# Down products of two FFN blocks in one PSUM group: one read-out for two blocks, two sets of operands

## The chip, the cores and the metric

The kernel runs on one core of one Trainium2 chip. The metric is the device time of one execution in microseconds (us); the median of several runs is quoted. The core's engines are TensorE (PE in the profile, with its weight loads shown apart as PEld), VectorE (DVE), ScalarE (ACT), GpSimd (POOL) and SyncE (SP, which here only issues DMAs). Each engine works through its own queue in order, and waits in it for semaphores of the others.

## The reference, cut to what matters

A trunk of two layers over 1024 positions and 1024 channels. Each layer first mixes tokens (Fourier groups, a linear recurrence and neighbourhood attention, not touched here) and then runs a SwiGLU feed-forward network (FFN) whose gated result is added to x:

```
h = modulate(rms_norm(x, g_ffn[l]), sh2, sc2)
f = (silu(h @ w_ffn_gate[l]) * (h @ w_ffn_up[l])) @ w_ffn_down[l]
x = x + gt2 * f
```

The inner width is 2816, that is 22 blocks of 128. Block number f contributes the product of a 128-column slice of silu(gate) * up, called A below, with 128 rows of `w_ffn_down`.

## The kernel before, in words

x stands transposed in SBUF as 8 tiles of 128 channels by 1024 positions. Every fp32 matmul is made of three matmuls on operands that were split into a rounded high part (hi) and a remainder (lo): hi by hi, hi by lo, lo by hi (`mm3`). A split costs one ACT copy (hi) and one subtraction on DVE, or for some weights on POOL (lo).

**FFN, blocks 0 and 1** are computed plainly by 16 jobs (`e_job`) of 12 matmuls each; the last four of them call `e_hook` after every sixth matmul, eight times in all. Meanwhile DVE and ACT prepare combinations of the normalised input (`prep`), with temporaries in the tile FA2 of the pool "prep".

**FFN, blocks 2 to 21** get gate and up from seven products in place of eight (`p_job`, in the order p = 1, 5, 6, 2, 7, 3, 4): 7 jobs of 12 matmuls, 84 in a block. The weights of p = 5, 6, 7 and 3 are combinations that POOL makes of the raw gate weights (wg) and up weights (wu). A job's weights are combined and split three jobs ahead, into a ring of four slots. The raw weights of the next block are loaded by two DMAs of 512 KB, issued with the preparation of p = 4. After each job `after` adds the product's bank into temporaries on DVE; after p = 3 and p = 4 the two halves (512 positions each) of A are complete, and `a_split` splits them.

**The down products.** `hook` is called after every sixth matmul, 14 times in a block. At eight of these hooks it calls `down_pair(l, f, m)` for one of the eight 128-channel tiles m of x: six matmuls for the block before, three into each of two PSUM banks (one for each half of the positions), and then one `scalar_tensor_tensor` (L204) of 128 by 1024 on DVE that multiplies both banks by the gate gt2 and adds them to x. The bank pairs 0-1 and 2-3 take turns; banks 4 to 7 belong to the seven products. The pairs of block f - 1 run at hooks 2 to 6 and 8 to 10 of block f, so that gate matmuls and down matmuls alternate by sixes. A block thus has 84 + 48 = 132 matmuls. There is one set of operands, A and its counterpart DW (the split rows of `w_ffn_down`), in the pool "ffa"; A of block f is written over that of block f - 1 once the latter's pairs are through. The rows of `w_ffn_down` come in two DMAs of 256 KB a block (`dw_load`) through one raw buffer, and `dw_split` splits each. The pairs of block 0 run in `e_hook` and the first hooks of block 2, those of block 1 behind them. Blocks 20 and 21 have their down products after the loop (`down_tail`), which adds both blocks up in PSUM already; block 21 keeps its operands in HX.

**Beside it, in layer 0,** blocks 3 to 16 compute layer 1's modulation vectors in the background: at each hook `bg(1)` advances `half_steps` by one step, and two steps are one DMA of 256 KB of `w_ada` into a single buffer (L1479) and one multiply-and-reduce over it on DVE (L1481, called the reduce below). Seven such pairs fall in a block.

Only PE's order is that of the code. The queues of the other engines are put in order when the program is built, by priority and by when operands are expected.

## Time and profile before

| | |
|---|---|
| time, median of 3 runs | 2391.38 us (2387.48 to 2394.67) |
| the profiled execution's own time | 2383.19 us |
| its span | 2381.3 us |
| mean granted TensorE clock | 0.974 |
| PE, PEld busy | 2236.1 us (94%), 1792.0 us (75%) |
| DVE, ACT, POOL busy | 1861.6 us (78%), 972.5 us (41%), 779.2 us (33%) |

The span runs from the first to the last instruction of the profiled execution; its own time is 1.9 us longer. Shares are of the span. The FFN of layer 0 with its down products lies at about 550 to 1208 us of the span, that of layer 1 at about 1715 to 2359 us.

### The profile page before, as it was taken

How to read it: one execution, taken by the hardware profiler on the slowest of the kernel's cores; microseconds unless marked ns; L12 is line 12 of the kernel's file. 1: busy time of each engine (PE TensorE's matmuls, PEld its weight loads, DVE VectorE, ACT ScalarE, POOL GpSimd, SP SyncE). 2: the span in 40 equal slices, each digit the busy share in tenths (PEclk: the TensorE clock that was granted, in tenths of full speed). 3: DMA queues.
4: the chain of work that ended last, by engine and by line, in shares of the span. 5: the costliest groups of instructions: out<-in, count | busy, mean ns of one | idle time of the engine just before them, and what ended most of it. 6: DMA issues, size and time to landing. Idle time of an engine off the chain costs nothing.

```text
span 2381.3 us, 27260 instructions
## 1 busy us (share of the span) xinstructions
PE 2236.1 (94%) x9802; PEld 1792.0 (75%) x9802; DVE 1861.6 (78%) x2698; ACT 972.5 (41%) x1606; POOL 779.2 (33%) x570
## 2 busy tenths in 40 slices
PE   6887998999999999999989989899999999999996
PEld 4665876777777778788867777677778888888885
DVE  8888788788788888887765676987877777777775
ACT  5375475543222222222353746745422222222234
POOL 4224375202233333333230325740123233333333
PEclk9998999999999999999989999999999999999998
DMA  8323423321333333321221132323011111111112
GB/s 294 101 72 107 137 74 123 116 99 45 98 107 110 112 113 102 113 74 53 80 97 58 40 107 69 110 73 118 27 58 54 54 52 51 49 50 53 53 49 71
DMA packets 77423, 203.81 MB, mean 86 GB/s; under 512 B 8932, under 2 KB 13028, under 8 KB 77287
## 3 DMA queue, kind: packets, MB, share of 16 engines
q1 hardware_dynamic: 73540, 183.41, 23.8%
q10 hardware_dynamic: 3746, 18.66, 2.3%
q8 instruction: 77, 1.26, 0.2%
q14 instruction: 60, 0.48, 0.1%
HBM read 193.64 MB, written 8.39 MB: 85 GB/s over the span
## 4 chain that ended last, share of the span: by engine, by line
PE 71%; DVE 17%; issue 4%; ACT 3%; POOL 2%; DMA 2%; SPq 0%; POOLq 0%; ACTq 0%; DVEq 0%
PE psum L190 71%; DVE rounded L201 3%; DVE plain L201 2%; DVE plain L204 1%; DVE ffa_A L201 1%; DVE psum L885 1%; DVE plain L312 1%; DMA plain<-in_ada 1%; ACT plain L198 1%; DVE psum L201 1%; ACT rounded L198 1%; ACT ffa_A L198 1%; ACT lru_LF L198 1%; POOL plain L1576 1%; DVE lru_LF L693 1%
## 5 line engine op out<-in xcount | busy, mean ns | idle before, releaser
L190 PE MATMUL psum<-rounded 128*128 128x512 f32 (+2 forms) x4332 | 1061.2, 394 | 34.2 <-DVE rounded L201 9.7
L190 PEld LDWEIGHTS psum<-rounded 128*128 128x128 f32 (+1 forms) x4332 | 817.2, 191 | 212.9 <-DVE rounded L201 12.6
L204 DVE SCALAR_TENSOR_TENSOR plain<-psum,plain 128x1024 f32<-128x1024 f32 (+2 forms) x416 | 474.7, 1148 | 202.2 <-PE psum L190 199.9
L198 ACT ACTIVATE rounded<-plain 128x512 fp32r<-128x512 f32 (+3 forms) x428 | 283.6, 668 | 743.9 <-PE psum L190 643.5
L190 PE MATMUL psum<-ffa_A,ffa_DW 128*128 128x512 f32 (+1 forms) x2040 | 526.7, 392 | 15.7 <-DVE ffa_A L201 6.7
L1323 POOL TENSOR_TENSOR plain<-plain 128x512 f32<-128x512 f32 x160 | 224.4, 1403 | 735.9 <-DMA plain<-in_wu 384.7
L190 PEld LDWEIGHTS psum<-ffa_A,ffa_DW 128*128 128x128 f32 x2040 | 378.8, 189 | 112.7 <-DVE ffa_A L201 16.3
L190 PE MATMUL psum<-hx_HX,rounded 128*128 128x512 f32 x1488 | 382.9, 394 | 0.0
L190 PEld LDWEIGHTS psum<-hx_HX,rounded 128*128 128x128 f32 x1488 | 280.4, 188 | 62.1
L1339 POOL TENSOR_TENSOR rounded<-plain,rounded 128x512 fp32r<-128x512 f32 x120 | 172.2, 1435 | 289.3 <-ACT rounded L198 289.1
L201 DVE TENSOR_TENSOR plain<-psum,plain 128x512 f32<-128x512 f32 (+1 forms) x288 | 193.9, 686 | 23.7 <-PE psum L190 16.4
L201 DVE TENSOR_TENSOR rounded<-plain,rounded 128x512 fp32r<-128x512 f32 (+4 forms) x147 | 154.5, 1065 | 50.1 <-ACT rounded L198 47.4
L922 POOL TENSOR_TENSOR rounded<-qk_PE,rounded 128x512 fp32r<-128x512 f32 (+3 forms) x132 | 140.8, 1074 | 127.7 <-ACT rounded L198 92.2
L198 ACT ACTIVATE plain<-plain 128x512 f32<-128x512 f32 (+5 forms) x181 | 113.3, 634 | 90.5 <-DVE plain L201 52.9
L190 PE MATMUL psum<-rounded,v_V 128*65 128x512 f32 (+4 forms) x528 | 130.1, 361 | 13.5 <-ACT rounded L198 3.6
L201 DVE TENSOR_TENSOR plain<-plain 128x512 f32<-128x512 f32 (+5 forms) x156 | 134.3, 863 | 6.9 <-ACT plain L198 1.9
L190 PE MATMUL psum<-qk_QT 128*128 128x512 f32 (+8 forms) x432 | 109.6, 354 | 22.1 <-DVE plain L885 16.4
L1339 DVE TENSOR_TENSOR rounded<-plain,rounded 128x512 fp32r<-128x512 f32 x160 | 115.5, 722 | 5.4 <-ACT rounded L198 5.3
L190 PEld LDWEIGHTS psum<-rounded,v_V 128*65 128x65 f32 (+1 forms) x528 | 75.4, 152 | 52.0 <-POOL rounded L922 6.3
L201 DVE TENSOR_TENSOR psum<-psum,plain 128x256 f32<-128x256 f32 x240 | 97.7, 410 | 21.1 <-PE psum L190 14.3
L198 ACT ACTIVATE ffa_DW<-plain 128x512 fp32r<-128x512 f32 x84 | 53.0, 631 | 139.2 <-PE psum L190 137.4
L190 PEld LDWEIGHTS psum<-qk_QT 128*128 128x128 f32 (+1 forms) x432 | 75.4, 194 | 41.4 <-DVE plain L885 20.4
(128 smaller groups left out, 2046.0 us busy)
## 6 DMA issues: line engine op xcount, KB each, us to landing
plain<-in_ada SPq DMA_DIRECT2D x96, 256.0 KB, 2.7
plain<-in_wd SPq DMA_DIRECT2D x88, 256.0 KB, 2.5
plain<-in_wg SPq DMA_DIRECT2D x40, 512.0 KB, 3.5
plain<-in_wu SPq DMA_DIRECT2D x40, 512.0 KB, 3.7
plain<-in_ada SPq DMA_DIRECT2D x30, 512.0 KB, 3.5
start_AT<-in_ada SPq DMA_DIRECT2D x18, 512.0 KB, 5.7
plain<-in_bias_t ACTq DMA_DIRECT2D x12, 768.0 KB, 5.8
plain<-in_bias_s ACTq DMA_DIRECT2D x12, 736.0 KB, 4.2
```

Source lines behind the costliest of these rows:

```text
L190: self.nc.tensor.matmul(out=out, lhsT=lhsT, rhs=rhs, start=start, stop=stop)
L198: self.nc.scalar.activation(out=out, in_=in_, func=func, **kw)
L201: self.nc.vector.tensor_tensor(out=out, in0=a, in1=b, op=op)
L204: self.nc.vector.scalar_tensor_tensor(out=out, in0=a, scalar=s, in1=b, op0=op0, op1=op1)
L312: self.nc.vector.tensor_tensor_reduce(out=raw, in0=raw, in1=self.f(self.M0, U), op0=ALU.mult, op1=ALU.add, scale=1.0, scalar=0.0, accum_ou ...
L693: nc.vector.tensor_tensor_scan(out=t, data0=a, data1=i, initial=0.0, op0=ALU.mult, op1=ALU.add)
L885: self.nc.vector.tensor_tensor_reduce(out=s, in0=s, in1=self.f(bo, a * w).rearrange("p (a b) -> p a b", a=a), op0=ALU.add, op1=ALU.max, sc ...
L922: (self.nc.vector if PLAN[self.l]["lo"][self.step] else self.nc.gpsimd).tensor_tensor(out=pl, in0=p, in1=ph.bitcast(F32), op=ALU.subtract)
L1323: comb = lambda out, a, b, op=ALU.subtract: nc.gpsimd.tensor_tensor(out=out, in0=a, in1=b, op=op)
L1339: (nc.gpsimd if LO_ENG[p] else nc.vector).tensor_tensor(out=lo, in0=src, in1=hi.bitcast(F32), op=ALU.subtract)
L1576: self.nc.gpsimd.tensor_tensor(out=x, in0=x, in1=accs[0], op=ALU.mult)
```

## The change

The down products of two neighbouring blocks, an even one and the odd one behind it, now go into one accumulation group: `down_pair(l, f, m)` issues twelve matmuls (for each half of the positions three of block f and three of block f + 1 into the same bank) and one `scalar_tensor_tensor` for both blocks. All of a pair's work stands in the next even block, at its hooks 3 to 10 (4 to 11 in block 2); odd blocks have none. An even block then has 84 + 96 = 180 matmuls and an odd one 84. There are two sets of operands: A0 and DW0 for even blocks, A1 and DW1 for odd ones. A1 and DW1 take the place of FA2, which is now put at the other end of SBUF and given up at the first hook of block 2. The loads and splits of the `w_ffn_down` rows keep their number but move: an even block splits the first half of its own rows, and an odd block the first half of its own, the second half of the even block's and the second half of its own. Blocks 0 and 1 no longer have down products in `e_hook`.

```diff
-PAIRS = {2: 0, 3: 1, 4: 2, 5: 3, 6: 4, 8: 5, 9: 6, 10: 7}
+PAIRS = {i + 3: i for i in range(8)}, {i + 4: i for i in range(8)}
...
-        self.pp = self.open(f"prep{l}", FA2=(4 * U, F32))
+        self.pp = self.open(f"prep{l}", "right", FA2=(4 * U, F32))
...
-            self.ap = self.open(f"ffa{l}", A=(2 * U, F32R), DW=(2 * U, F32R))
+            self.ap = self.open(f"ffa{l}", A0=(2 * U, F32R), DW0=(2 * U, F32R))
...
-        if i >= 4:
-            self.down_pair(l, 0, i - 4)
-        if i == 4:
+        elif i == 4:
             self.dw_split(0, 1)
             self.dw_load(l, 1, 0)
-        elif i == 7:
-            self.dw_split(1, 0)
-            self.dw_load(l, 1, 1)
...
     def ad(self, f):
-        return (self.HX[:, :2 * U], self.HX[:, 2 * U:4 * U]) if f == NRUN - 1 else (self.A[:, :], self.DW[:, :])
+        if f == NRUN - 1:
+            return self.HX[:, :2 * U], self.HX[:, 2 * U:4 * U]
+        return (self.A1, self.DW1) if f % 2 else (self.A0, self.DW0)
...
     def down_pair(self, l, f, m):
         d = self.fd()
         for j, n in enumerate(NS):
-            self.down(f, m, n, self.bank(d + j), True, True)
+            for i in range(2):
+                self.down(f + i, m, n, self.bank(d + j), not i, i == 1)
...
         if f == FIRST:
-            if i < 4:
-                self.down_pair(l, 0, 4 + i)
-            if i == 3:
-                self.dw_split(1, 1)
+            if i == 0:
+                self.shut(self.pp)
+                self.pp = self.open(f"ffb{l}", "right", A1=(2 * U, F32R), DW1=(2 * U, F32R))
+                self.dw_split(1, 0)
+                self.dw_load(l, 1, 1)
+            elif i == 1:
                 for half in range(2):
                     self.e_split(1, half)
                 self.free.append(self.ea[1, 0])
+            elif i == 2:
+                self.dw_split(1, 1)
                 self.dw_load(l, f, 0)
-            m = i - 4
-            prev = 1
-        else:
-            m = PAIRS.get(i, -1)
-            prev = f - 1
+        elif f % 2 == 0:
             if i == 0:
                 self.dw_load(l, f, 0)
...
+        m = -1 if f % 2 else PAIRS[f == FIRST].get(i, -1)
+        if m >= 0:
+            self.down_pair(l, f - 2, m)
             if m == 3:
                 self.dw_split(f, 0)
-                self.dw_load(l, f, 1)
-            if m == 7:
-                self.dw_split(f, 1)
-        if self.late and i >= LATE:
+                self.dw_load(l, f + 1 if f + 1 < NRUN - 1 else f, f + 1 == NRUN - 1)
+        if f % 2 and f < NRUN - 1:
+            if i in (1, 5, 9):
+                self.dw_split(f - (i == 5), i > 1)
+                if i < 9:
+                    self.dw_load(l, f - (i == 1), 1)
```

## Rows read from the trace of the kernel before

**Rows 1.** The page: busy time, share of the span, instructions of two engines
```profile
PE 2236.1 (94%) x9802; PEld 1792.0 (75%) x9802; DVE 1861.6 (78%) x2698; ACT 972.5 (41%) x1606; POOL 779.2 (33%) x570
```

**Rows 2.** Windows: eleven blocks of layer 0, eleven of layer 1, block 21 of layer 0
```profile
core 0: us, PE busy (x) PEld busy (x) DVE busy (x) ACT busy (x) POOL busy (x), PEclk, DMA share, GB/s
671.15:1015.65 344.50, 338.97 (x1452) 271.96 (x1453) 297.31 (x442) 93.66 (x155) 112.51 (x77) 1.00 0.35 110
1829.90:2162.60 332.70, 332.70 (x1453) 271.84 (x1452) 248.88 (x276) 94.59 (x155) 105.63 (x77) 1.00 0.17 53
1163.55:1182.81 19.26, 19.26 (x86) 15.78 (x84) 12.36 (x17) 9.41 (x14) 3.36 (x3) 1.00 0.40 123
```

**Rows 3.** Waits of PE, 671.15 to 1015.65, then 1710 to 2320 (total us, times, longest)
```profile
PE psum L190 <- ACT ffa_A L198: 3.0, 11, 0.5
PE psum L190 <- DVE ffa_A L201: 2.5, 11, 0.3
...
PE psum L190 <- DVE ffa_A L201: 1.9, 2, 1.2
PE psum L190 <- DVE plain L204: 1.7, 1, 1.7
```

**Rows 4.** Timeline of PE: first down matmuls of blocks 4 and 7, layer 0
```profile
638.29 0.50 PE L190 MATMUL psum<-ffa_A,ffa_DW 128*128 128x512 f32 x1 [1.67 <-ACT ffa_A L198]
639.02 1.61 PE L190 MATMUL psum<-ffa_A,ffa_DW 128*128 128x512 f32 x5 [0.22 <-DVE ffa_A L201]
640.43 2.76 PE L190 MATMUL psum<-hx_HX,rounded 128*128 128x512 f32 x6
642.99 1.79 PE L190 MATMUL psum<-ffa_A,ffa_DW 128*128 128x512 f32 x6
...
733.75 0.50 PE L190 MATMUL psum<-ffa_A,ffa_DW 128*128 128x512 f32 x1 [0.24 <-ACT ffa_A L198]
734.47 1.42 PE L190 MATMUL psum<-ffa_A,ffa_DW 128*128 128x512 f32 x5 [0.22 <-DVE ffa_A L201]
```

**Rows 5.** Timeline of DVE at the end of one block, layer 0
```profile
761.10 0.68 DVE L201 TENSOR_TENSOR plain<-psum,plain 128x512 f32<-128x512 f32 x1
761.88 1.00 DVE L201 TENSOR_TENSOR ffa_A<-plain,ffa_A 128x512 fp32r<-128x512 f32 x1
762.80 1.77 DVE L201 TENSOR_TENSOR plain<-plain 128x512 f32<-128x512 f32 x1
764.50 0.68 DVE L1481 CUSTOM_DVE_ANT_0 plain<-plain 128x512 f32<-128x512 f32 x1
...
765.27 0.69 DVE L201 TENSOR_TENSOR ffa_A<-plain,ffa_A 128x512 fp32r<-128x512 f32 x1
```

**Rows 6.** Groups of DVE, 671.15 to 1015.65 (count | busy us, mean ns | idle before)
```profile
L204 DVE SCALAR_TENSOR_TENSOR plain<-psum,plain 128x1024 f32<-128x1024 f32 x88 | 112.1, 1280 | 17.2 <-PE psum L190 17.0
L1481 DVE CUSTOM_DVE_ANT_0 plain<-plain 128x512 f32<-128x512 f32 x77 | 58.3, 758 | 21.4 <-DMA plain<-in_ada 20.8
```

**Rows 7.** Two reduces in a row on DVE; landing times of the DMAs before them
```profile
737.18 0.69 DVE L1481 CUSTOM_DVE_ANT_0 plain<-plain 128x512 f32<-128x512 f32 x1 [1.76 <-DMA plain<-in_ada]
...
740.45 0.69 DVE L1481 CUSTOM_DVE_ANT_0 plain<-plain 128x512 f32<-128x512 f32 x1 [0.18 <-DMA plain<-in_ada]
...
DMA to landing us min/median/max: 2.4/2.7/3.5
```

**Rows 8.** Timeline of PE, then DVE, while blocks 0 and 1 end, layer 0
```profile
553.18 1.44 PE L190 MATMUL psum<-ffa_A,ffa_DW 128*128 128x512 f32 x5 [0.65 <-DVE ffa_A L201]
...
565.91 1.63 PE L190 MATMUL psum<-ffa_A,ffa_DW 128*128 128x512 f32 x6 [1.66 <-DVE plain L204]
...
579.57 0.72 PE L190 MATMUL psum<-ffa_A,ffa_DW 128*128 128x512 f32 x2 [1.22 <-DVE ffa_A L201]
...
566.29 1.39 DVE L201 TENSOR_TENSOR rounded<-prep_FA,rounded 128x512 fp32r<-128x512 f32 x1
```

**Rows 9.** Timelines of ACT, SP and POOL: raw up weights on their way, layer 0
```profile
742.66 0.64 ACT L198 ACTIVATE rounded<-plain 128x512 fp32r<-128x512 f32 x1 [4.89 <-PE psum L190]
...
748.17 0.33 SPq L1258 DMA_DIRECT2D plain<-in_wu  x1
...
752.45 3.13 POOL L1323 TENSOR_TENSOR plain<-plain 128x512 f32<-128x512 f32 x2 [13.31 <-DMA plain<-in_wu]
755.54 1.29 POOL L1339 TENSOR_TENSOR rounded<-plain,rounded 128x512 fp32r<-128x512 f32 x1
```

More of the change, by code (lines that the diff above doesn't have):

```diff
@@ L152, in __init__, with open @@
         self.queue, self.look, self.sq = deque(), 1, {}
-    def open(self, name, **tiles):
-        cm = self.tc.tile_pool(name=name, bufs=1)
+    def open(self, name, side="left", **tiles):
+        cm = self.tc.tile_pool(name=name, bufs=1, side=side)
         pool = cm.__enter__()
```

18 lines of the change are left out of this document (9 added, 9 removed).

## Prediction

> **What bounds the kernel now.** I read the page's engine shares first. PE is busy 94% of the span and DVE 78% [rows 1]: PE is the bound, and DVE work costs time only where PE waits for it. The change takes no matmul away, so anything it brings must come out of PE's waits. So the next view was PE's waits, one FFN at a time.
>
> The windows say where they are. Eleven whole blocks of layer 1 take 332.70 us with PE busy in all of it, that is 30.25 us a block. Eleven of layer 0 take 344.50 us, 31.32 us a block, with the same number of matmuls and the full granted clock [rows 2]. Layer 0 loses 1.07 us a block. The waits name the place: eleven times PE waits for ACT's and eleven times for DVE's half of the split of A [rows 3], at the first down pair of a block. The timeline shows one such place: 0.24 and 0.22 us idle, and the matmuls behind them start late as well [rows 4]. DVE's timeline shows why A is late: add the last product (761.10), split the other half, a multiplication that takes 1.77 us, then a background reduce at 764.50, and the last subtraction ends at 765.96 [rows 5]. Layer 1 has no reduces and no such wait.
>
> So the places where the change can pay are the entries of layer 0's blocks 4 to 16, thirteen of them, and the start of each FFN, where PE idles 0.65, 1.66 and 1.22 us in layer 0 [rows 8] and 3.6 us in layer 1 [rows 3].
>
> **What is removed.** Eight pairs for two blocks instead of sixteen: 80 fewer evacuations a layer, 160 in all, at 1.280 us [rows 6], 205 us of DVE. In layer 1 this hides entirely behind PE, which never waited in its steady blocks: worth 0 there.
>
> **What moves: the entries of blocks.** A of an even block f is now needed two blocks later, so the six entries of odd blocks (5 to 15) lose their wait. At an even block's entry A of the odd block before is still needed, but later: at hook 3 instead of 2 (6 matmuls), and behind 3 matmuls of the even block's half, 9 matmuls at 0.229 us (332.70 us over 1453, [rows 2]) or 2.06 us. The present loss is 1.07 us, so 1.0 us is to spare.
>
> What the 13 entries cost now: twelve at 1.07 are 12.8 us. The first (block 4) is dearer: 1.67 us idle; then 2.14 us from 638.29 to 640.43, and 2.56 from there to 642.99, for six matmuls each that take 1.37 elsewhere [rows 4]: 1.67 + 0.77 + 1.19 = 3.6. Together 16.4 us.
>
> **What is added: odd blocks without cover.** An odd block has only its 84 matmuls. Block 21 of layer 0 is such a block in the present trace: 19.26 us, PE busy throughout [rows 2], but without reduces and without a next block's weights. That is 0.229 us a matmul, so alternating with down matmuls costs nothing that its end would give back. DVE's work in an odd block of layer 0 is 297.31 / 11 = 27.0 us less eight evacuations (10.2), plus a third `w_ffn_down` split (0.7, like the subtraction at 765.27, [rows 5]): 17.5 us of 19.26. To that come waits for the w_ada DMAs, 20.8 / 11 = 1.9 us a block now [rows 6]: 19.4 us, just full.
>
> These waits can grow. The reduces come every second hook, 12 matmuls or 2.75 us in an odd block; two in a row can't start closer than about 3.27 us (737.18 to 740.45, where the second waited for its DMA, which needs 2.4 us at the least, [rows 7]). Seven need 22.9 us, 3.6 more than the block has. How much of this delays A depends on whether DVE stands waiting in its queue or has other work first. Bounds for the added wait at each of the seven even entries (4, 6, ... 16): below, all absorbed, 0; above, all 3.6 us less the 1.0 to spare, 2.6 us, 18.2 in all. With the waits of today A would be 0.1 us late, inside the slack; with twice the waits, 21.3 us, 2.0 us late, 1.0 beyond it. I take the middle, 0.5 us, 3.5 in all: reduces now mostly run behind other work, as the one at 764.50 did. Layer 0's entries then give 16.4 - 3.5 = 12.9 us (bounds 16.4 and -1.8).
>
> **The multiplication** of 1.77 us [rows 5] reads two SBUF operands while the add of the same size from PSUM takes 0.68. The Trainium skill's page "SBUF — State Buffer", section "Who interferes with whom", says that a DVE instruction with two SBUF inputs contends with a GpSimd instruction that reads SBUF, and one with a single SBUF input does not; the trace agrees with 1.77 against 0.68. By that rule the evacuations never disturbed POOL, so removing them frees nothing there, while the same POOL work in a shorter odd block meets DVE's two-input work more often: another multiplication drawn out by 1.1 us each time would be 7.7 us over seven blocks, within the bounds above.
>
> **Start of each FFN.** The down pairs of block 0 leave the stretch at 552 us, so the three waits (0.65, 1.66, 1.22 us) lose their place: block 0's A has five more hooks, the 1.66 us for a late evacuation [rows 8] has no evacuation left to wait for, and A1 isn't written over A0, which put the 1.22 us there. Late next is A1 and DW1 themselves: they lie where FA2 was, and the preparation reads FA2 until 567.7 (566.29 plus 1.39, [rows 8]). Without the three evacuations in that stretch of DVE it would end at 567.7 - 3 x 1.28 = 563.9. From 552.2, the hook of the first pair now, to the new first pair at hook 4 of block 2 lie eight groups of six gate matmuls, 1.37 us each: 563.1, and 563.8 behind the three matmuls of A0. A split of DW1 and one of A1 follow the release: 2 x 0.69 on DVE behind 0.64 on ACT, 565.9 at the latest. Wait 0 to 2.1 us, taken as 1.0. Each layer saves 3.5 to 3.6 less 1.0: 2.5, two layers 5.0 us (bounds 2.9 and 7.1).
>
> **At nothing:** the loads keep their number and size (256 KB each for `w_ffn_down`) and their raw buffer has 12 or more matmuls between uses, 2.75 us against the 2.4 to 2.7 us that DMAs of this size take [rows 7]; uncovered, each would cost ACT 1 to 2 us in its queue, ahead of weight splits that are made three jobs (8.2 us) early. A bank pair is used again two hooks later, 5.5 us with gate work, against 1.28 us for the evacuation. The tail is unchanged.
>
> **Sum.** 12.9 + 5.0 = 17.9 us. From the profiled execution's own 2383.2 us this makes 2365.3. That execution was 8.2 us quicker than the median of the runs, 2391.4; on that scale the forecast is 2373.5 us, 0.75% less.
>
> **Rivals.**
> 1. *All absorbed.* DVE keeps up in odd blocks, and A1 is in time: 16.4 + 7.1 = 23.5 us, 2368. For it: evacuations are 10.2 of DVE's 27.0 us a block. Against it: 17.5 of 19.26 us are still booked, with waits to come.
> 2. *The reduces take the place of the evacuations.* All 2.6 us at the seven entries: layer 0 gives -1.8, the starts 5.0; 3.2 us gained, 2388: no change. For it: 1.76 us of such waiting stands in the trace with two evacuations ready behind it or nearly so [rows 7]. Close to it is the case that nothing at all is gained, 2391: PE is busy 94%, and work is taken from an engine that isn't the bound. The Trainium skill's page "Perfetto Trace Analysis", section "Identifying the Most-Contended Engine", says to find the engine with the highest occupancy and to optimise that one first; by that rule a cut in DVE's work gives 0. The trace disagrees in part: PE waits for DVE at the places counted above.
> 3. *The weights become late in odd blocks: slower.* The raw up weights of the next block can be asked for only when p = 4 of this one is split. Now that split begins at 742.66 on ACT, the DMA is issued at 748.17, 5.5 us later, and POOL has combined and split the first product from them by 756.83, 8.7 us after that [rows 9]. In an odd block the split can begin after three jobs, 8.2 us in; 8.2 + 5.5 + 8.7 = 22.4 us, and PE wants it at 19.26 + 2.75 = 22.0. It decides as soon as the DMA goes out later than 13.3 us into an odd block. If the 3.6 us by which the reduces lag come on top, PE waits 4.0 us in each of seven blocks: 28.0 us lost, against 17.9: 10.1 us slower, 2401.5. Against it: the 5.5 us hold evacuations that are gone from odd blocks; each is 1.28.
>
> **How the numbers follow.** Forecast 0.50, rival 1 0.18, rival 2 with its neighbour 0.21, rival 3 0.11. About 0.3% (7.2 us) is what a measurement of this kernel can tell from no change; the three runs of before lie as far apart. Faster 0.68, same 0.21, slower 0.11. The likeliest case's own range is 2368 to 2382 (the wait at even entries between 0 and 1.4 us, A1's between 0 and 2.1). The range of 2365 to 2393 reaches over rivals 1 and 2 and leaves out rival 3 and the edges.
>
> **What would show it.** Right: 160 fewer evacuations; no wait for A at odd entries of layer 0; even entries with under 1 us; PE's start waits below 1.1 us a layer; pairs of blocks in layer 0 at 60.5 to 62 us, in layer 1 unchanged at 60.5. Wrong: PE waiting for weight splits (`rounded`) of the first products of even blocks would be rival 3; waits for A of 2 us and more at even entries, with DVE idle for w_ada before them, rival 2. A new order of the queues that holds up something I didn't look at would make it wrong in either direction.

## The result, and the profile after

The changed kernel takes 2402.73 us, median of 7 runs (2396.42 to 2405.36), against 2388.54 us (2384.50 to 2394.67, 7 runs) of the kernel before: ratio 1.0058, 95% interval 1.0046 to 1.0070. It is slower by 14 us; a gain of 0.75% was forecast.

The profiled execution has an own time of 2400.51 us, 17.3 above that of before. Matched matmul by matmul, 5.6 us of this lie ahead of 550 us, where both kernels issue the same matmuls: from 510.8 us TensorE's granted clock stands at 1.2 GHz for 13.7 us, in the execution of before for 3.4 us. Both lengths turn up in executions of either layout, so this part is not the change's. The start of layer 0's FFN wins 0.5 us, 11.8 are lost in layer 0's blocks 3 to 16, and all that follows comes to 0.4.

The page's engine line, to be held against [rows 1]:
```profile
PE 2247.8 (94%) x9802; PEld 1805.0 (75%) x9802; DVE 1689.2 (70%) x2538; ACT 965.0 (40%) x1606; POOL 780.0 (33%) x570
```
DVE has 160 instructions and 172 us less; PE as many matmuls as before. The windows of ten blocks of layer 0 (from the entry of block 6, its first down matmul, to that of block 16) and ten of layer 1, against [rows 2]:
```profile
core 0: us, PE busy (x) PEld busy (x) DVE busy (x) ACT busy (x) POOL busy (x), PEclk, DMA share, GB/s
698.05:1019.30 321.25, 310.77 (x1321) 252.00 (x1320) 236.39 (x370) 84.55 (x141) 103.43 (x71) 0.98 0.36 110
1867.59:2170.46 302.87, 302.81 (x1322) 247.78 (x1320) 178.75 (x211) 83.70 (x142) 95.79 (x70) 1.00 0.17 53
```
Layer 1 takes 60.57 us for two blocks, as before (60.5). Layer 0 takes 64.25, where before had 62.64: each even entry now costs 3.68 us, against 2.14 for two entries before. Of the 18.38 us that layer 0 takes more than layer 1 here, 10.48 are idle PE; 7.9 are not idle, and the clock column shows 0.98.

PE's waits in 580 to 1060 us, then in layer 1, against [rows 3]:
```profile
PE psum L190 <- ACT ffb_A L198: 14.5, 7, 3.3
PE psum L190 <- DVE ffb_A L201: 1.8, 6, 0.7
...
PE psum L190 <- ACT ffb_A L198: 1.6, 1, 1.6
PE psum L190 <- DVE ffb_A L201: 1.2, 1, 1.2
```
Odd blocks have no wait left, as forecast. The seven even ones wait 16.3 us, all for `ffb_A`, the A1 of the odd block before. Layer 1 waits only at its start, 2.8 us where it was 3.6. PE's timeline at the entry of block 12 (some expectations below call it block 10's), against [rows 4], and the windows of the same place:
```profile
889.53 0.86 PE L190 MATMUL psum<-ffa_A,ffa_DW 128*128 128x512 f32 x3
893.04 1.95 PE L190 MATMUL psum<-ffb_A,ffb_DW 128*128 128x512 f32 x3 [2.64 <-ACT ffb_A L198]
894.78 1.49 PE L190 MATMUL psum<-ffa_A,ffa_DW 128*128 128x512 f32 x3
...
890.00:893.00 3.00, 0.39 (x2) 0.00 (x0) 2.93 (x7) 0.65 (x2) 0.37 (x1) 1.00 0.74 191
893.00:896.50 3.50, 3.46 (x8) 2.43 (x9) 1.81 (x3) 1.51 (x3) 1.27 (x1) 0.52 0.39 136
896.50:900.00 3.50, 3.50 (x17) 2.86 (x16) 2.17 (x5) 0.00 (x0) 0.00 (x0) 1.00 0.27 75
```
The wait has two prices. PE idles 2.64 us, and when it starts again the granted clock is 0.52 for 3.5 us, near the lower level of 1.2 GHz: 8 matmuls in place of 17, another 1.7 us. Six of the seven entries have such a half-clock stretch of 3.4 us right behind the wait (waits of 1.7 to 3.5 us); the seventh, block 8's, with a wait of 1.6 us, has none. Four of the six lie in the window of ten blocks: 6.8 of the 7.9 us that were not idle. The Trainium skill's page "TensorE: Matmul & The Clock Gate", section "Part 1: The HAM clock gate (the "warmup" mystery)", says that the gate halves the clock of an engine that has been idle and that activity releases it; the trace agrees, with 0.52 behind the wait and 1.00 after it.

Why A1 is late: DVE's, ACT's, POOL's and SP's timelines at the end of odd block 11, against [rows 5, 9]. PE finished p = 4 of block 11 about 24 matmuls before 889.53, at 884.0:
```profile
874.18 0.69 DVE L1484 CUSTOM_DVE_ANT_0 plain<-plain 128x512 f32<-128x512 f32 x1 [2.83 <-DMA plain<-in_ada]
...
875.40 0.68 DVE L1334 TENSOR_TENSOR rounded<-plain,rounded 128x512 fp32r<-128x512 f32 x1
...
886.22 0.69 DVE L1334 TENSOR_TENSOR rounded<-plain,rounded 128x512 fp32r<-128x512 f32 x1 [1.45 <-ACT rounded L198]
886.83 0.69 DVE L201 TENSOR_TENSOR plain<-plain 128x512 f32<-128x512 f32 x1
887.43 1.79 DVE L1484 CUSTOM_DVE_ANT_0 plain<-plain 128x512 f32<-128x512 f32 x1
...
889.26 1.13 DVE L201 TENSOR_TENSOR plain<-plain 128x8 f32<-128x8 f32 x1
890.32 0.68 DVE L201 TENSOR_TENSOR ffb_A<-plain,ffb_A 128x512 fp32r<-128x512 f32 x1
890.92 0.68 DVE L201 TENSOR_TENSOR plain<-psum,plain 128x512 f32<-128x512 f32 x1
...
893.02 0.69 DVE L201 TENSOR_TENSOR ffb_A<-plain,ffb_A 128x512 fp32r<-128x512 f32 x1
...
885.55 0.64 ACT L198 ACTIVATE rounded<-plain 128x512 fp32r<-128x512 f32 x1 [3.81 <-POOL plain L1318]
886.09 0.61 ACT L198 ACTIVATE plain<-plain 128x512 f32<-128x512 f32 x1
...
892.35 0.63 ACT L198 ACTIVATE ffb_A<-plain 128x512 fp32r<-128x512 f32 x1 [3.65 <-DVE plain L201]
...
879.77 2.68 POOL L1318 TENSOR_TENSOR plain<-plain 128x512 f32<-128x512 f32 x2 [7.19 <-DMA plain<-in_wu]
...
876.11 0.33 SPq L1258 DMA_DIRECT2D plain<-in_wu  x1
```
The add of that last product stands at 890.92: DVE takes it 6.9 us after PE has finished it. In [rows 5], before, DVE took it at 761.10, within a microsecond of PE. Ahead of it in DVE's queue now stand the weight subtraction of p = 6, the gating of the other half, a reduce that takes 1.79 us beside POOL, a tiny addition of 1.13 us and the other half's split. The subtraction waits for ACT, ACT for POOL's combination, POOL for the up weights, whose DMA went out at 876.11, 11.3 us into the block. It goes out when the subtraction of p = 4's weights (875.40) has ended, and that stood behind a reduce which had waited 2.83 us for w_ada.

How many reduces stand in such a block shows in the windows of their instructions alone, over block 11 and block 12 (the count in brackets takes each reduce and the read of its sum apart):
```profile
core 0: us, DVE busy (x), PEclk, DMA share, GB/s
864.79:884.05 19.26, 3.35 (x8) 1.00 0.40 124
884.05:929.89 45.84, 8.75 (x22) 0.96 0.34 103
```
The forecast had seven reduces in every block. In this execution each odd block from 5 to 15 has four and each even one from 4 to 14 eleven, as DVE's queue was ordered. DVE is busy for 14.7 of the 19.26 us of an odd block and waits 3.4 for w_ada (means of blocks 5 to 15).

DVE's groups over the same ten blocks, against [rows 6]:
```profile
L1484 DVE CUSTOM_DVE_ANT_0 plain<-plain 128x512 f32<-128x512 f32 x75 | 62.8, 837 | 38.6 <-DMA plain<-in_ada 38.3
L204 DVE SCALAR_TENSOR_TENSOR plain<-psum,plain 128x1024 f32<-128x1024 f32 x40 | 51.2, 1280 | 13.9 <-PE psum L190 13.8
```
Half the evacuations (L204, the read-out of a bank pair) per block, at 1.280 us as before. A reduce is dearer (837 ns against 758), and DVE waits 3.8 us a block for w_ada where it waited 1.9: less work means that DVE comes to the reduce before its data. Last, the start of layer 0's FFN, against [rows 8]: PE, then ACT and DVE.
```profile
571.79 0.50 PE L190 MATMUL psum<-ffb_A,ffb_DW 128*128 128x512 f32 x1 [1.61 <-ACT ffb_A L198]
573.49 0.73 PE L190 MATMUL psum<-ffb_A,ffb_DW 128*128 128x512 f32 x2 [1.20 <-DVE ffb_A L201]
...
566.89 0.63 ACT L198 ACTIVATE rounded<-plain 128x512 fp32r<-128x512 f32 x1 [3.45 <-POOL plain L1318]
...
567.55 0.69 DVE L1334 TENSOR_TENSOR rounded<-plain,rounded 128x512 fp32r<-128x512 f32 x1 [1.86 <-ACT rounded L198]
...
569.36 1.19 DVE L201 TENSOR_TENSOR rounded<-prep_FA,rounded 128x512 fp32r<-128x512 f32 x1
```
The last read of FA2 ends at 570.55, not at 563.9 as forecast: the same chain, POOL to ACT to DVE, stands ahead of it. A1 and DW1, which lie where FA2 was, come 2.8 us late.

### The profile page after: what moved, and what is told of

Its sections match the earlier page's. It is cut to its first block, busy times and chain, and to the rows that moved or that the text cites. A ratio compares the mean times of both kernels' runs of the same rounds, so it can differ in the third digit from the quotient of the medians.

```text
span 2398.7 us, 27154 instructions
## 1 busy us (share of the span) xinstructions
PE 2247.8 (94%) x9802; PEld 1805.0 (75%) x9802; DVE 1689.2 (70%) x2538; ACT 965.0 (40%) x1606; POOL 780.0 (33%) x570
## 4 chain that ended last, share of the span: by engine, by line
PE 65%; DVE 20%; issue 4%; POOL 4%; DMA 4%; ACT 3%; SPq 0%; POOLq 0%; DVEq 0%; ACTq 0%
PE psum L190 65%; DVE rounded L201 3%; DVE plain L201 2%; POOL plain L1318 2%; DVE plain L204 2%; DMA plain<-in_ada 1%; DMA plain<-in_wu 1%; DVE plain L312 1%; DVE psum L885 1%; ACT plain L198 1%; ACT rounded L198 1%; DVE rounded L1334 1%; DVE plain L1484 1%; DVE psum L201 1%; ACT lru_LF L198 1%
## 5 line engine op out<-in xcount | busy, mean ns | idle before, releaser
L190 PE MATMUL psum<-rounded 128*128 128x512 f32 (+2 forms) x4332 | 1052.3, 393 | 33.6 <-DVE rounded L201 10.3
L204 DVE SCALAR_TENSOR_TENSOR plain<-psum,plain 128x1024 f32<-128x1024 f32 (+2 forms) x256 | 270.1, 1063 | 152.1 <-PE psum L190 151.9
L190 PE MATMUL psum<-hx_HX,rounded 128*128 128x512 f32 x1488 | 365.3, 393 | 0.0
L190 PE MATMUL psum<-ffa_A,ffa_DW 128*128 128x512 f32 (+1 forms) x1080 | 304.7, 393 | 0.7 <-ACT plain L198 0.7
L190 PE MATMUL psum<-ffb_A,ffb_DW 128*128 128x512 f32 x960 | 281.5, 400 | 22.0 <-ACT ffb_A L198 17.7
L190 PEld LDWEIGHTS psum<-ffa_A,ffa_DW 128*128 128x128 f32 x1080 | 204.2, 191 | 44.6 <-ACT plain L198 1.5
L190 PEld LDWEIGHTS psum<-ffb_A,ffb_DW 128*128 128x128 f32 x960 | 182.3, 192 | 71.2 <-ACT ffb_A L198 21.6
L201 DVE TENSOR_TENSOR rounded<-plain,rounded 128x512 fp32r<-128x512 f32 (+4 forms) x147 | 153.8, 1060 | 50.2 <-ACT rounded L198 47.3
L1484 DVE CUSTOM_DVE_ANT_0 plain<-plain 128x512 f32<-128x512 f32 x96 | 79.2, 825 | 52.6 <-DMA plain<-in_ada 47.1
```

The source lines that it names most:

```text
L190: self.nc.tensor.matmul(out=out, lhsT=lhsT, rhs=rhs, start=start, stop=stop)
L201: self.nc.vector.tensor_tensor(out=out, in0=a, in1=b, op=op)
L204: self.nc.vector.scalar_tensor_tensor(out=out, in0=a, scalar=s, in1=b, op0=op0, op1=op1)
L1484: self.nc.vector.tensor_tensor_reduce(out=raw, in0=raw, in1=self.f(self.M0 + i * HALF, HALF), op0=ALU.mult, op1=ALU.add, scale=1.0, scalar ...
```

## The experiments

Every experiment was timed in five rounds beside the kernel before (median 2387.2 to 2388.8 on these chips); ratios are to it, with 95% intervals. Theory 1, in its first form: the background (DMAs of w_ada and reduces) makes A1 late, by way of DVE's queue. Its rivals: the moved order alone, or the fewer evacuations. Diffs are against the changed kernel unless they name the kernel before.

**Without the w_ada DMAs.** The DMA is left out, and the reduce multiplies the vector with itself, so layer 1's modulation is another.
```diff
-                    self.nc.sync.dma_start(out=raw, in_=self.I["ada"][l, 8 * c + j, :, i * HALF:i * HALF + HALF])
...
-                        out=raw, in0=raw, in1=self.f(self.M0 + i * HALF, HALF), op0=ALU.mult, op1=ALU.add,
-                        scale=1.0, scalar=0.0, accum_out=self.f(part[i] + j, 1))
+                        out=raw, in0=self.f(self.M0 + i * HALF, HALF), in1=self.f(self.M0 + i * HALF, HALF), op0=ALU.mult, op1=ALU.add,
+                        scale=0.001, scalar=0.0, accum_out=self.f(part[i] + j, 1))
```


> The changed kernel without the background's w_ada DMAs: each reduce multiplies the broadcast vector by itself, so DVE does the same work and waits for no DMA (layer 1's modulation is then not the reference's). Theory 1 (in odd blocks DVE stands in its queue for w_ada): the waits for A at layer 0's even entries, 16.3 us in the changed kernel, fall below 4 us in all, the half-clock stretches behind them go, and the time falls by 18 to 28 us, to 2375 to 2385. Theory 2 (an odd block is too short for POOL's weight combinations and for DVE's work beside them, DMAs or not): at least 1.2 us stay at each of the seven entries and the time falls by less than 10 us, to 2393 or more.

> The kernel before with the same omission of the w_ada DMAs, as the base for the run above. Theory 1: the wait of about 1 us at thirteen entries comes from the reduces' DVE time and from their DMAs; without the DMAs some of it stays: 4 to 14 us less than before, 2374 to 2385, level with the changed kernel under the same omission or up to 6 us above it. Theory 2: the changed kernel stays at least 8 us above this one.


Measured: 2403.13 us, 1.0060 (1.0044 to 1.0076), and with the same edit in the kernel before 2402.28, 1.0062 (1.0049 to 1.0075). The first has theory 2's time but not its waits at all seven entries; the second missed both. Without DMAs to wait for, the queue was built with all 96 reduces bunched into blocks 3 to 8 (3 to 9 in the kernel before), and PE waits for A there (up to 5.0 us at an entry in the one, 3.3 in the other) and nowhere behind. Taking the DMAs away made the kernel before 13 us slower: the pair says nothing about the DMAs, but shows that it counts where the reduces stand, with their number unchanged.

**Half the evacuations alone.** In the kernel before, odd blocks' products are not added to x; nothing is moved.
```diff
-        self.stt(x, self.PS[:, d:d + 2, :], self.f(self.mod[l] + 40 + m, 1), x, ALU.mult, ALU.add)
+        if f % 2 == 0:
+            self.stt(x, self.PS[:, d:d + 2, :], self.f(self.mod[l] + 40 + m, 1), x, ALU.mult, ALU.add)
```


> The kernel before with the down products' scalar_tensor_tensor left out for odd blocks (their contribution to x is missing), and nothing moved: the fewer evacuations alone. If evacuations are what makes A late at the entries of layer 0's blocks, as the forecast had it, the thirteen waits go and the time falls by 12 to 18 us, to 2371 to 2377. If A is late because of what stands directly ahead of it on DVE (the reduce and the multiplication), evacuations earlier in the block don't matter: 0 to 6 us less, 2383 to 2389.


Measured: 2407.59, 1.0081 (1.0069 to 1.0093): 19 us slower with 160 instructions less; both ranges missed. In the profiled executions layer 0's FFN loses 12 us and layer 1's 10. Layer 1, which had no steady waits, has them now at entries (waits of PE from 1700 us on, and DVE's timeline at one entry):
```profile
PE psum L190 <- DVE ffa_A L201: 3.7, 10, 1.2
PE psum L190 <- ACT ffa_A L198: 1.8, 8, 0.2
...
1965.97 0.69 DVE L201 TENSOR_TENSOR ffa_A<-plain,ffa_A 128x512 fp32r<-128x512 f32 x1 [0.70 <-ACT ffa_A L198]
1966.58 0.68 DVE L201 TENSOR_TENSOR plain<-psum,plain 128x512 f32<-128x512 f32 x1
```
Where the evacuations are gone, the queue has the late half's split, which waits 0.70 us for ACT, ahead of the last product's add; in the blocks with evacuations the add comes first. Eight entries idle 0.45 us each so, and the matmuls behind start late as in [rows 4]; the other 1.9 us of the first line are those of the start, as before. Fewer instructions gave another order, and the order cost time. In layer 1 there is no background that could do it.

**The move with all evacuations.** Two groups and two evacuations a pair, everything else as in the changed kernel.
```diff
-        for j, n in enumerate(NS):
-            for i in range(2):
-                self.down(f + i, m, n, self.bank(d + j), not i, i == 1)
+        for i in range(2):
+            d = self.fd()
+            for j, n in enumerate(NS):
+                self.down(f + i, m, n, self.bank(d + j), True, True)
...
+            self.stt(x, self.PS[:, d:d + 2, :], self.f(self.mod[l] + 40 + m, 1), x, ALU.mult, ALU.add)
```


> The changed kernel with two groups and two evacuations in each of its pairs, as many as before: the move into even blocks alone. Theory 1 and theory 2: even blocks have air on DVE (41 us for some 37 us of work with 16 evacuations), so it costs at most a few us beside the changed kernel: 2400 to 2409, with the same waits for A at even entries. If the fewer evacuations do help the changed kernel, this one is slower than it by 8 us or more.


Measured: 2410.69, 1.0090 (1.0075 to 1.0105), 8 us above the changed kernel and a little above the range. In this layout the halved evacuations are worth 8 us (with all of them, PE waits 11.1 us for banks); the move itself costs more than that.

**No background at all,** in the changed kernel and in that of before; layer 1's modulation is set to 0.01.
```diff
-            self.steps = self.half_steps([(1, c) for c in ((1, 0, 2, 4, 3, 5) if NRUN == NFF or STOP == 1 else (1, 0))])
+            self.nc.vector.memset(self.f(self.mod[1], 48), 0.01)
+            self.steps = None
```


> The changed kernel with the whole background of layer 0's FFN left out (no w_ada loads, no reduces; layer 1's modulation is a constant 0.01, not the reference's). Theory 1 (the reduces and their DMAs, sitting in DVE's queue in odd blocks, make A late): layer 0 then runs like layer 1, no wait for A at block entries, no half-clock stretches between 600 and 1060 us; about 25 us less than the changed kernel, 2374 to 2382. Theory 2 (the short odd block is too tight for POOL and DVE by itself): waits of 1 us and more stay at even entries, 2393 or more.

> The kernel before with the background left out in the same way, as the base. Theory 1: its thirteen waits of about 1 us go: 12 to 17 us less than before, 2372 to 2378; the changed kernel without the background lies within 5 us of it, because nothing is left for fewer evacuations to give. Theory 2: it lies 10 us or more below the changed kernel without the background. A third theory (any edit of DVE's work makes the builder order its queue anew, and the order, not the amount, decides): it comes out slower than 2382 although work was only taken away.


Measured: 2377.03, 0.9948 (0.9935 to 0.9961), as theory 1 had it, and 2367.67, 0.9918 (0.9902 to 0.9933), below its range. In the changed kernel PE has no wait at all from 640 to 1180 us, and matched matmul by matmul the two profiles keep their distance over all steady blocks. So the loss in layer 0's steady blocks needs the background. The medians still stand 9.4 us apart. Part of that is the start: the waits of 1.6 and 1.2 us are there in both layers, and in this execution the clock falls behind them, as the windows of both starts show (0.74 and 0.87):
```profile
569.00:582.00 13.00, 10.20 (x31) 7.58 (x30) 9.60 (x11) 3.72 (x7) 4.10 (x3) 0.74 0.29 84
1720.00:1733.00 13.00, 10.22 (x36) 7.42 (x35) 10.50 (x13) 4.39 (x8) 4.78 (x3) 0.87 0.28 88
```
Matched matmul by matmul, the two profiled executions lie 7.0 us apart: 3.3 ahead of 558 us, 2.8 by the start of layer 0's FFN, 1.8 at block 4's entry (1.2 us of waiting), 1.2 at layer 1's start, and -2.1 in all else. So the starts, forecast as a gain, cost time here. Stretches at half clock ahead of the FFN vary from execution to execution; what they add to the distance of the medians isn't shown.

The run also shows how the background makes A1 late. DVE and ACT at the end of the same block 11, whose last matmul ends at 872.8:
```profile
873.03 0.69 DVE L1334 TENSOR_TENSOR rounded<-plain,rounded 128x512 fp32r<-128x512 f32 x1 [2.15 <-ACT rounded L198]
...
875.95 0.68 DVE L201 TENSOR_TENSOR plain<-psum,plain 128x512 f32<-128x512 f32 x1
...
877.77 0.63 ACT L198 ACTIVATE ffb_A<-plain 128x512 fp32r<-128x512 f32 x1 [2.25 <-DVE plain L201]
```
The subtraction of p = 6 begins 0.3 us behind the block's end, with the background 2.2; from there to ACT's copy of A1's first half it is 4.7 us, with it 6.1, in which two reduces stand. Over the seven entries A1's first half is copied 2.4 us earlier on average: 1.3 because p = 6's operand is there earlier, 1.1 because the way from it to A1 is shorter.

**The background in even blocks,** and the same with the even block's six matmuls of a pair issued ahead of the odd block's.
```diff
-            self.bg(1)
+            if f % 2:
+                self.bg(1 if i in (4, 8) else 0)
+            else:
+                self.bg(2 if 2 <= i <= 11 else 1 if i in (1, 12) else 0)
```
and, in the second of them,
```diff
-        for j, n in enumerate(NS):
-            for i in range(2):
+        for i in range(2):
+            for j, n in enumerate(NS):
                 self.down(f + i, m, n, self.bank(d + j), not i, i == 1)
```


> The changed kernel, all of its work kept, with the background moved: one pair of load and reduce in an odd block (hooks 4 and 8), eleven in an even one (hooks 1 to 12), against seven in each. Theory 1: waits for A at layer 0's even entries fall from 16.3 us to below 5 us in all and the half-clock stretches behind them go; 15 to 25 us less than the changed kernel, 2377 to 2388. Theory 2: no gain above 6 us, 2396 or more.

> As the run above, and each down pair does the even block's six matmuls (both halves of the positions) before the odd block's six, so that PE asks for the odd block's A 0.7 us later and its second half no earlier. Theory 1: whatever wait is left at an even entry shrinks by up to 0.7 us, 0 to 5 us less than the run above over nine entries in each layer and two starts; 2374 to 2386. If A is late by a lot more than 0.7 us for another reason, no difference.


Measured: 2401.21, 1.0058 (1.0044 to 1.0072), and 2386.08, 0.9993 (0.9983 to 1.0003). The first did not test what it was meant to: in blocks 4 to 15 each odd block still had four reduces and each even one eleven, the numbers of the changed kernel itself, because DVE's queue is ordered by when the DMAs are expected, one pair in 3.2 us and more. So it can't speak for theory 2, in whose range it lies. The second gained 15 us over the first where 0 to 5 were expected. A1's first half is needed 3 matmuls or 0.7 us later, the five entries from block 8 on wait 0.4 to 0.7 us for ACT, and one half-clock stretch of 3.4 us is left from 600 us on, in place of six.

**The order of a pair's matmuls alone** (the second diff above), and with the pairs one hook later as well.
```diff
-        m = -1 if f % 2 else PAIRS[f == FIRST].get(i, -1)
+        m = -1 if f % 2 else PAIRS[1].get(i, -1)
```


> The changed kernel with one edit: a down pair issues the six matmuls of the even block first and then the six of the odd block, so that the odd block's A is needed behind 9 instead of 3 matmuls of the pair... that is three matmuls of 0.229 us later for its first half. The background is as in the changed kernel. Theory 1 (lateness of A, plus a stretch at half the granted clock that a wait of over about 2 us draws behind it): the seven waits, 2.4 us on average, lose 0.7 us each (4.8 us) and fall below 2 us, so most of the six half-clock stretches (1.7 us each) go as well: 2388 to 2393 us, some 10 to 15 below the changed kernel. Theory 2 (the gain of the run with the background in even blocks came from both edits together; the order alone is worth its three matmuls): 2397 to 2399.

> The changed kernel, the even block's six matmuls of a pair first, and the eight pairs at hooks 4 to 11 of every even block instead of 3 to 10 (as block 2 has them already). The odd block's A is then needed 0.7 + 1.4 = 2.1 us later than in the changed kernel. Theory 1 (the lateness of A is all that costs in the steady blocks): the waits of 1.2 to 3.5 us shrink to 0.3 us on average, no half-clock stretch is left between 600 and 1180 us: the 12 us that layer 0's blocks lost against the kernel before are won back, and some of the 16 us that its entries cost there too: 2375 to 2384 us, faster than both. Rival: what stands later (A0's and DW0's release, the preparation of the next block) turns into a new wait, or the even block's A is late for a bank: 2388 or more.


Measured: 2390.66, 1.0004 (0.9994 to 1.0015), and 2394.75, 1.0023 (1.0011 to 1.0035). The order alone wins 12 us of the 14 back, inside theory 1's range, so an A1 that comes late, with the clock behind it, is most of the loss. PE's waits from 720 us on (blocks 8 to 16) in that run:
```profile
PE psum L190 <- ACT ffb_A L198: 3.6, 5, 1.0
PE psum L190 <- DVE ffb_A L201: 1.1, 5, 0.2
```
These five waits are 1.3 us shorter on average than in the changed kernel: 0.7 for the later need, and 0.6 because A1 comes earlier, for here the DMA of the up weights goes out 9.8 to 9.9 us into the odd block (10.2 to 11.3 in the changed kernel). At blocks 4 and 6 that DMA goes out at 13.7 and 12.6, the subtraction of p = 6 begins over 4 us behind the odd block's end, and PE waits 3.8 and 3.9 us, longer than in the changed kernel. 10.2 us at half clock are left of 20.5.

The later hook missed theory 1: A1 is needed 1.4 us later again, but six entries wait 1.5 to 2.6 us for it. The hook also moves the evacuations and one split of `w_ffn_down` towards the odd block, and A1 comes later by more than the time won.

**Half of the background, in even or in odd blocks.** Three of layer 1's six vectors are computed, the rest is set to 0.01; the steps run in even blocks alone, or in odd blocks alone.
```diff
-            self.steps = self.half_steps([(1, c) for c in ((1, 0, 2, 4, 3, 5) if NRUN == NFF or STOP == 1 else (1, 0))])
+            self.nc.vector.memset(self.f(self.mod[1], 48), 0.01)
+            self.steps = self.half_steps([(1, 1), (1, 0), (1, 2)])
...
-            self.bg(1)
+            self.bg(1 - f % 2)
```
(and `self.bg(f % 2)` in the other).


> The changed kernel; three of layer 1's six modulation vectors are computed, the others are set to 0.01. The background steps run at the hooks of even blocks alone, seven pairs of DMA and reduce a block, from block 4 to 16; odd blocks have none. Theory 1 (the reduces in the odd blocks, 19 us long, make A late): steady entries of layer 0 wait under 0.5 us each, no half-clock stretch behind them, and the time is that of the changed kernel without any background, 2377 us, within 4. Theory 2 (any background in layer 0, the load of DMAs or the reduces in even blocks, does it): waits of 1.2 us or more stay at half of the entries, 2387 or more.

> The counterpart: the same three of six vectors, with the background steps at the hooks of odd blocks alone, seven pairs a block, from block 3 to 15. Theory 1: at each of the even entries 4 to 16 the wait for A stays at 1.2 us or more, with half-clock stretches behind the longest, and the time stays within 6 us of the changed kernel: 2396 to 2403, though half of the reduces are gone. Theory 2 (any background does it): halfway between the changed kernel and the one without background, 2385 to 2392.


Measured: 2386.52, 0.9987 (0.9974 to 1.0001), and 2389.09, 0.9998 (0.9987 to 1.0009). Again the steps were not where the code has them: in both runs all 48 reduces ran between 616 and 820 us, four in each odd block from 5 to 9 and eleven in blocks 4, 6 and 8, as in the changed kernel. So odd and even blocks could not be told apart, and that the second time lies in theory 2's range decides nothing. What they show is a before and after in one execution: the four entries up to 830 us wait 1.1 to 3.5 us, and PE has no wait from 840 to 1180 us, where the reduces have ended.

**The subtraction that DVE waits for, on POOL.** It is that of p = 6 for an even block, made at the end of the odd block before; alone, with the order of the matmuls, and, for all blocks, in the kernel before.
```diff
-            (nc.gpsimd if LO_ENG[p] else nc.vector).tensor_tensor(out=lo, in0=src, in1=hi.bitcast(F32),
+            (nc.gpsimd if LO_ENG[p] or p == 6 and l == 0 and f % 2 == 0 else nc.vector).tensor_tensor(out=lo, in0=src, in1=hi.bitcast(F32),
```


> The changed kernel with one subtraction moved: the remainder of p = 6's weights of odd blocks of layer 0, prepared at the end of the even block before? no: of the even blocks 2 to 20, whose split falls at the end of the odd block before, is made by POOL, which has just combined them, and no longer by DVE. In the changed kernel DVE stands in its queue for that operand (1.45 us before block 10) with the additions and subtractions of the odd block's A behind it. Theory 1 (that wait is what makes A late): the seven waits of 2.4 us on average fall to 1 us and less, the half-clock stretches behind them go, block 4 apart: 2385 to 2392 us. Theory 2 (the reduces and their DMAs make A late, that wait only stands beside them): waits of 2 us and more stay, 2398 to 2404.

> The same subtraction on POOL and, as well, the even block's six matmuls ahead of the odd block's in each pair. Theory 1: what is left of the waits after the order of the matmuls alone (0.7 to 1.2 us at five entries, 4 us at two) goes too, 2378 to 2385 us, faster than the kernel before. Theory 2: no better than the order of the matmuls alone, 2388 to 2393.

> The control: the kernel before, with that subtraction on POOL for all blocks of layer 0. In its trace DVE comes to this subtraction only behind the last part of A or without a wait ahead of it, so by theory 1 nothing is to be gained: 2385 to 2392 us. If it gains 5 us or more, the subtraction is a burden anywhere, and no cause of the change's loss. If it loses, POOL's longer chain is what costs.


Measured: 2404.63, 1.0073 (1.0056 to 1.0090); 2396.45, 1.0033 (1.0021 to 1.0046); 2389.45, 1.0001 (0.9989 to 1.0014). Theory 1 in that form fell: nothing gained, with the order 6 us lost. ACT's and DVE's timelines at the same place say why:
```profile
887.23 0.63 ACT L198 ACTIVATE rounded<-plain 128x512 fp32r<-128x512 f32 x1 [3.81 <-POOL plain L1318]
887.77 0.61 ACT L198 ACTIVATE plain<-plain 128x512 f32<-128x512 f32 x1
...
888.41 1.37 DVE L201 TENSOR_TENSOR plain<-plain 128x512 f32<-128x512 f32 x1 [1.97 <-ACT plain L198]
```
DVE waits as long for the silu instead, since ACT stands in its own queue for POOL's combination with the silu behind it. The late operand blocks two queues, and taking it off one doesn't help.

**The up weights asked for earlier.** The subtraction of p = 4 in layer 0's odd blocks, which releases their DMA, goes from DVE, where it stands behind a reduce that waits for w_ada, to POOL, which is idle; alone and with the order of the matmuls.
```diff
-            (nc.gpsimd if LO_ENG[p] else nc.vector).tensor_tensor(out=lo, in0=src, in1=hi.bitcast(F32),
+            (nc.gpsimd if LO_ENG[p] or p == 4 and l == 0 and f % 2 else nc.vector).tensor_tensor(out=lo, in0=src, in1=hi.bitcast(F32),
```


> The changed kernel with another subtraction moved: in layer 0's odd blocks the remainder of p = 4's weights is made by POOL, which stands idle for 7 us there, and no longer by DVE, where it waits behind a reduce. The DMA of the next block's up weights is released by it and so goes out some 2 to 3 us earlier. Theory 1 (the chain DMA, POOL's combinations, ACT's copy for p = 6, and behind that in ACT's queue the silu, sets when the odd block's A begins): A comes 1.5 to 3 us earlier, the seven waits of 2.4 us fall to 1 us and less, the half-clock stretches behind them go: 2384 to 2392 us. Theory 2 (DVE's own queue with reduces, 1.8 us beside POOL, between the last additions, sets when A ends): waits of 1.8 us and more stay, 2396 to 2404.

> The same, and the even block's six matmuls ahead of the odd block's in each pair. Theory 1: hardly a wait is left but at block 4, 2378 to 2386 us, faster than the kernel before. Theory 2: as with the order of the matmuls alone, 2388 to 2393.


Measured: 2394.26, 1.0026 (1.0014 to 1.0039), and 2382.87, 0.9986 (0.9974 to 0.9997). Alone it wins 8 us: short of the 11 to 19 of theory 1, more than theory 2 allowed. But it did not do what it was meant to: POOL makes the subtraction from 9.0 to 10.3 us into the odd block, and the DMA goes out at 10.3 to 11.3 in blocks 5 to 15, no earlier than in the changed kernel (10.2 to 11.3). So the gain says nothing about the chain of the up weights. PE's waits for A at the seven entries come to 13.2 us in place of 16.3, up to 3.3 at one entry and now for DVE's half of the split as well; three half-clock stretches lie behind them in place of six, 5.1 us less. With the order it is the fastest complete version, 0.7% or 17 us under the changed kernel by the ratios and just under the kernel before, by 0.14%. Theory 1 gave that time, for a reason that the trace doesn't bear out. PE's waits, 580 to 1180 us:
```profile
PE psum L190 <- ACT ffb_A L198: 5.3, 3, 4.4
PE psum L190 <- DVE ffb_A L201: 2.7, 5, 0.7
```
4.9 of the 8.0 us are those of block 4.

**Shorter reduces.** Each reduce reads 128 of 512 columns, so three quarters of the modulation's products are left out; the DMAs stay whole.
```diff
-                        out=raw, in0=raw, in1=self.f(self.M0 + i * HALF, HALF), op0=ALU.mult, op1=ALU.add,
+                        out=raw[:, :HALF // 4], in0=raw[:, :HALF // 4], in1=self.f(self.M0 + i * HALF, HALF // 4), op0=ALU.mult, op1=ALU.add,
```


> The changed kernel with each reduce over 128 of the 512 columns; the other three quarters of layer 1's modulation products are left out, the DMAs stay whole. Theory 1 (the DMA's landing and the chain of the up weights count, since DVE waits for w_ada all the same): waits of 1.5 us and more stay at most entries, 2394 to 2403. Theory 2 (DVE's time in the reduces counts): each entry loses the 0.5 us of a reduce, and 1.3 us where one meets POOL, so waits of 1 us and less, without half-clock stretches: 2382 to 2391.


Measured: 2378.95, 0.9966 (0.9952 to 0.9979), below what either theory gave. PE's waits from 640 us on, and the same part of DVE's queue:
```profile
PE psum L190 <- ACT ffb_A L198: 0.9, 1, 0.9
PE psum L190 <- DVE ffb_A L201: 0.9, 4, 0.2
...
878.19 0.69 DVE L1334 TENSOR_TENSOR rounded<-plain,rounded 128x512 fp32r<-128x512 f32 x1 [3.51 <-ACT rounded L198]
...
879.40 1.39 DVE L1484 CUSTOM_DVE_ANT_0 plain<-plain 128x128 f32<-128x128 f32 x1
```
DVE still waits for ACT and POOL at this place, and even longer (3.51 us), and still waits for w_ada, yet PE waits only 1.8 us in all. At the entries of blocks 8 to 14 DVE's instructions stand in the order of the changed kernel, so here it is their time that counts. It acts in two ways of like size: over the seven entries the operand of p = 6 is there 0.9 us earlier (the DMA goes out 0.5 us earlier on average), and the way from it to A1 is 0.9 us shorter. Which of the two is the larger, no run separates.

## Why the prediction was wrong, point by point

*Removed evacuations:* right. 160 instructions at 1.28 us are gone, and layer 1 gains nothing from it.

*Odd entries:* right. Their waits are gone.

*The added wait at even entries* is the step that failed: "1.0 us is to spare", 0.5 us each taken, 2.6 at most, 3.5 in all. Measured are 16.3 us idle at seven entries, 2.3 each, and six half-clock stretches that cost 1.7 us each: 26.5 us against the 16.4 that all thirteen entries cost before, 10.1 of the 11.8 us lost in these blocks. Two errors are in it. The first is the booking: 19.4 of 19.26 us of DVE time in an odd block was held to mean that A is 0.1 us late. Its terms were wrong: seven reduces in 17.5 us of work, and 1.9 of waiting, where the run has four in 14.7 and 3.4. And such a sum knows no order. What A hangs on lies behind the odd block's end: the last product's add came 6.9 us after PE. The run without background shows what fills that time, in about equal parts. DVE waits for the operand of p = 6, late because DVE's wait for w_ada delays the up weights' DMA; and two reduces stand between it and A. With the background gone, or ended in the second half of the runs with half of it, the waits go too.

The second error is the price. The forecast charged a wait at its idle time. [rows 4] already held the rest: six matmuls in 2.14 and 2.56 us where 1.37 is usual, right behind a wait of 1.67 us. They were booked as a peculiarity of block 4; the window around them has a granted clock of 0.71, a half-clock stretch of before:
```profile
638.20:644.00 5.80, 5.48 (x16) 4.14 (x17) 3.29 (x5) 1.67 (x4) 0.43 (x1) 0.71 0.44 151
```
The idle time alone, 16.3 us, lies inside the bound of 18.2; with 1.7 us behind six of the seven waits it doesn't, and that is why the range didn't hold the time. It is also why the order of the matmuls won 12 us with 4.0 us less waiting over the seven entries: five of them came from 2.2 us on average to 0.9, and half of the half-clock time went.

*The multiplication beside POOL:* right in kind. At the entry shown not the multiplication but the reduce (1.79 against 0.68 us) and a 128 by 8 addition (1.13 against 0.17) are drawn out, ahead of A's first half. The 7.7 us were left inside the bounds and not in the sum.

*Starts of the FFNs:* mis-sized. 2.5 us a layer were forecast from a wait of 1.0, at most 2.1; the wait is 2.8, and the gain 0.7 to 0.8. FA2 was taken to be free at 563.9, by taking evacuations out of DVE's time; it was free at 570.55, since DVE stood for the p = 6 weights there as well. In time, the start of layer 0's FFN wins 0.5 us in the profiled execution; without the background, where the clock falls behind this wait, it costs 2.8.

*At nothing:* right. The `w_ffn_down` loads and the bank pairs showed no wait of PE, nor did the down products of blocks 20 and 21 in layer 0.

*The rivals:* the loss is rival 2's place (waits for A of 2 us and more at even entries, DVE idle for w_ada before them) at a higher price. Rival 3's chain is there too, but not where it was looked for: the DMA went out 11.3 us into the block, inside its 13.3, and PE never waited for weights; the queues of ACT and DVE did, with A behind. Rivals 2 and 3 were priced as alternatives, and they came together.

*Open:* the runs don't separate a reduce in the odd block from one in the even block behind it, as the queue moved them, nor what won the 8 us when p = 4's subtraction went to POOL: the trace has another order of DVE's queue and fewer half-clock stretches. Why the clock differs ahead of the FFN between executions wasn't tried.

## What to carry to other kernels

Taking work off an engine that isn't the bound helps only if what the bound waits for comes earlier, and in an in-order queue that is a matter of what stands ahead of it: look up at what time the queue reaches the one instruction that the bound waits for, not how full the engine is. Price a wait of TensorE with what follows it: matmuls that run slow right behind a wait are part of its cost, and a reordering that brings the wait down can pay more than the time it moves. Where queues are ordered when the program is built, look in the trace where the instructions stand before an experiment on them is believed: here two edits that were meant to move reduces, and one that was meant to send a DMA out earlier, left them where they were. Run a removal by itself first: here less work, with nothing else changed, cost 19 us.

## What had not been expected of the hardware

Waits of 1.7 to 3.5 us were enough for the granted clock to fall to 1.2 GHz for 3.4 us, again and again in the middle of a kernel whose mean clock is 0.967. The length of the wait alone doesn't say whether it falls: it fell behind 1.7 us (block 6), and not behind 1.6 us (block 8) nor behind 2.5 us at block 10 of the run with the pairs one hook later. The 128 by 8 addition on DVE, 0.17 us elsewhere, took 1.13 us beside POOL, and a reduce a quarter as long still took 1.39 us there (0.29 elsewhere): what is drawn out beside POOL grows by about 1 us, whatever the instruction's size.
